# Two small unused tiles shift the places of a weight ring in SBUF

## The chip, the cores and the metric

The kernel runs on one core of one Trainium2 chip. The metric is the device time of one launch in microseconds (us). Before the change it is 1526.59 us, the median of three runs (1525.78 to 1528.01). The execution that the profiler recorded took 1525.17 us, of which the recorded span of instructions is 1523.3 us.

## The reference

Two residual layers act on x, 256 tokens of 1024 channels in float32. Each layer has a token mixer and a channel mixer. In layer 0 the channel mixer is a dense SwiGLU, in layer 1 it is a sum over eight experts of which each token uses two:

```
for l in range(DEPTH):                                   # 2 layers
    ada = cs @ ada_w[l] + ada_b[l]                       # six vectors that scale and shift
    h = rmsnorm(x, norm_mix_g[l]) * (1.0 + sc1) + sh1
    x = x + g1 * token_mixer(h, ...)                     # recurrence and attention, 9 projections
    h = rmsnorm(x, norm_ffn_g[l]) * (1.0 + sc2) + sh2
    f = swiglu(h, w1, w3, w2) if l % 2 == 0 else moe_swiglu(h, router, w1, w3, w2)
    x = x + g2 * f
...
for e in range(N_EXPERTS):                               # in moe_swiglu
    out = out + comb[:, e:e + 1] * swiglu(t, w1[e], w3[e], w2[e])
```

An expert has two matrices of 1024 x 3584 and one of 3584 x 1024, together 42 MB (here and below one MB of a load is 1024 KB, as the profile's list of DMAs counts). All eight are read once: 336 MB of the weights that the kernel reads.

## The kernel before

Every weight passes through a ring of buffers in SBUF and is read from there by TensorE. A load is one DMA of 1 MB into a place of 8192 bytes on each of the 128 partitions; `load` (lines 115 to 124) issues it from SyncE's queue. In the layers before the experts the ring is the pool `rawp` with 6 places (`RAW_BUFS`, line 33), and `split` (line 132) turns each tile into a high and a low part `wh` and `wl`, which are places of 4096 bytes in the pool `splp`.

In the expert stage (`moe`, line 757) nothing is split. The ring has 16 places there (line 1040), which `ahead` (line 1042) fills in a fixed rotation:

- places 0 to 5: the 6 places of `rawp`, here called the first ring;
- places 6 to 10: 5 places `raw2` of the expert stage's own pool, the second ring (`RAW_MORE`);
- place 11: the two tiles `xT`, which hold half a load each;
- places 12 to 15: the 4 + 4 places of `wh` and `wl`, again half a load each.

```
slots_ = RAW_BUFS + RAW_MORE + 1 + SPLIT_BUFS                         # line 1040
src, turn_ = plan[len(loaded)](), len(loaded) % slots_                # line 1045
halves = [xt.rearrange("p k t -> p (k t)") for xt in xT]              # line 1049, place 11
halves = [splp.tile([P, 1024], F32, tag=tag, ...) for tag in ("wh", "wl")]  # line 1051, places 12 to 15
load(src, raw, k=k)                                                   # line 1057, a whole load
nc.sync.dma_start(half.rearrange("p (k f) -> p k f", k=k // 2), part) # line 1063, a half load
```

So a row of the profile with SyncE's line L120 is a whole load into one of the two rings, and L1063 is a half load (or the two halves of the last unit).

An expert is worked in four units. Units 0 to 2 take 1024 columns of the hidden width, unit 3 takes 512. A unit's `up` (line 1074) reads 8 loads (unit 3: 4) of the first two matrices and `down` (line 1121) reads 4 loads (unit 3: 2) of the third. What stands in one unbroken run of bytes differs: an `up` load of units 0 to 2 brings runs of 4096 bytes, one of unit 3 runs of 2048 bytes, and a `down` load runs of 8192 bytes, or 4096 where it is cut into halves. An expert thus has 24 loads of 4096-byte runs, 4 of 2048 and 14 of 8192. Half of the experts are held for up to 96 tokens, half for up to 64 (`CAPS`, line 35). An expert of 96 tokens needs a third group of matmuls for each load (L1092, L1138); one of 64 does not.

The order of the work is this. SyncE issues the loads in the order of `plan` (line 1030). It waits for TensorE to release the place of 16 loads earlier, and no more than 8 DMAs stand in the queue, since 8 semaphores tell of landings in turn. TensorE consumes the loads in the same order. Which engine waits is decided by whether the next load has landed.

The places themselves come from the order in which tiles and pools are made. The pool `const` lies first, then `keep`, `hp`, `gp`, `rawp`, `splp`, and behind these the pools of the single stages.

Of the kernel before, what the change touches and what calls it, by code (L numbers as in the profile page):

```python
# [8 lines left out]
F32 = mybir.dt.float32  # L9
# [8 lines left out]
P = 128  # L18
# [30 lines left out]
def hybrid_trunk(ctx: ExitStack, tc: tile.TileContext, x, c, ada_w, ada_b, norm_mix_g, norm_ffn_g, w_in, lb_logits,  # L49
# [7 lines left out]
    const = ctx.enter_context(tc.tile_pool(name="const", bufs=1))  # L57
# [14 lines left out]
    def nm(s):  # L72
        uid[0] += 1
        return f"{s}_{uid[0]}"
# [18 lines left out]
    def ms():  # L93
        return msp.tile([P, 512], F32, tag="ms", name=nm("ms"))
# [6 lines left out]
    def small(shape, name, dt=F32, bufs=None, pool=None):  # L101
        return (pool or phase[0]).tile(shape, dt, tag=name, name=nm(name), **({"bufs": bufs} if bufs else {}))
# [56 lines left out]

    xT = [const.tile([P, 4, S], F32, name=f"xT{h}") for h in range(2)]  # L160
    ident = const.tile([P, P], F32, name="ident")
    cT = const.tile([P, KD], F32, name="cT")
    nc.sync.dma_start(cT, c.rearrange("o (p k) -> (o p) k", k=KD))
    first_phase = ExitStack()
# [592 lines left out]
    def moe(y, l, pdp):  # L757
# [12 lines left out]
        nc.sync.dma_start(row, ada_b[l, 4096:].rearrange("(q f) -> q f", q=4).unsqueeze(1).broadcast_to((4, 32, 512)))  # L770
        v_.tensor_tensor(row, row, ada[l, 2]["row"], op=ALU.add)
        lp = [ms() for _ in range(NT)]
        xs = [small([P, D], "xs") for _ in range(NT)]
        begun = set()
        xg = [small([P, D], "xg") for _ in range(NT)]
# [481 lines left out]
    for l in range(DEPTH):  # L1257
# [23 lines left out]
        if l % 2 == 0:  # L1281
            with new_phase("ffn"):
                gain = pcol[:, R_FFN + 8 * l:R_FFN + 8 * l + 8]
                sc, sh = ada[l, 2]["col"][:, 0:8], ada[l, 1]["col"][:, 8:16]
                early, then = unnormed(gain, sc, sh)
                acc = end_of_mixer(then)
                queue(*QUEUES[2 * l + 1])
                if l == 0:
                    fillers.append(late_constants)
                filling[:] = -DELAYS[2 * l + 1], RATES[2 * l + 1]  # L1290
                rb = in_sbuf(norm_rows(acc))
                acc, early = dense_ffn(early, rb, lambda: norm_T(rb, gain, sc, sh), l)
                while fillers:
                    fillers.pop(0)()
        else:
            before_experts.close()
            turn_mm[0] = -(1 << 30)
            with tc.tile_pool(name="pdp", bufs=2, space=PSUM) as pdp, new_phase("moe"):
                moe(y, l, pdp)
# [57 lines left out]
```

## Time and profile before

| what | value |
|---|---|
| median of 3 runs | 1526.59 us |
| profiled execution | 1525.17 us, its span 1523.3 us |
| TensorE (PE) busy | 1470.4 us, 97% of the span |
| VectorE (DVE), ScalarE (ACT) busy | 629.3 us (41%), 373.9 us (25%) |
| DMA | 506.62 MB (10^6 bytes) in 186032 packets, mean 333 GB/s |
| share of the chain that ended last | PE 83%, DMA 9%, issue 5% |

The span has four parts. Up to about 34 us the first scale and shift vectors are formed. From there to about 600 us stand the layers' projections, which TensorE does nearly without a gap at about 240 GB/s of DMA. To about 668 us follow the last projection and the router. From 668 to 1510 us the experts run: TensorE is nearly full and the DMA engines move about 410 GB/s all the while. An engine's busy time counts each matmul with a modelled end, so a short wait of TensorE may show as busy.

### The profile page before, as it was taken

What the parts mean: (1) busy time and instruction counts of PE and PEld (TensorE: products, weight loads), DVE (VectorE), ACT (ScalarE), POOL (GpSimd) and SP (SyncE); (2) the same over time, 40 slices, a digit from 0 to 9 for tenths busy, and PEclk for the clock granted to TensorE, in tenths of its full rate; (3) what the DMA queues carried; (4) which work ended last, traced back from release to release, by engine and by line L of the source; (5) the groups of instructions that cost most, each with busy time, mean ns of one, the idle gap of its engine ahead of it and who ended that gap; (6) DMA issues with size and microseconds to landing.
All of it is one profiled execution on the core that took longest, in us unless ns stands there. A gap on an engine that the chain in (4) does not pass through costs nothing.

```text
span 1523.3 us, 29680 instructions
## 1 busy us (share of the span) xinstructions
PE 1470.4 (97%) x12659; PEld 893.8 (59%) x12659; DVE 629.3 (41%) x1046; ACT 373.9 (25%) x618; POOL 33.9 (2%) x34
## 2 busy tenths in 40 slices
PE   5999999999999999999999999999999998999996
PEld 3988999999998899863333333433334332234322
DVE  4898777877688887631100211120011120111202
ACT  3535556544455455310000000000000000000000
POOL 1010100000000100000000000000000000000000
PEclk7999999999999999899999999999999999999999
DMA  9988545678896555868999999999999999999996
GB/s 356 369 303 282 189 139 166 222 237 302 267 342 227 194 178 200 293 229 321 408 412 413 410 416 411 415 415 410 410 415 411 412 417 408 413 406 409 412 416 250
DMA packets 186032, 506.62 MB, mean 333 GB/s; under 512 B 11016, under 2 KB 79252, under 8 KB 170148
## 3 DMA queue, kind: packets, MB, share of 16 engines
q1 hardware_dynamic: 185572, 504.56, 86.7%
q8 instruction: 101, 1.65, 0.4%
q14 instruction: 39, 0.32, 0.1%
q0 software_dynamic: 320, 0.09, 0.0%
HBM read 503.56 MB, written 1.05 MB: 331 GB/s over the span
## 4 chain that ended last, share of the span: by engine, by line
PE 83%; DMA 9%; issue 5%; DVE 1%; SPq 1%; ACT 1%; POOL 0%; DVEq 0%; POOLq 0%; ACTq 0%
PE mm L157 31%; PE mm L1087 23%; DMA raw<-in_moe_w_dram 8%; PE pd L1132 6%; PE at L1092 6%; PE pd L1138 4%; PE at L1132 4%; PE ms L862 2%; PE ms L530 2%; DMA raw<-in_ada_w_dram 1%; PE ms L1114 1%; PE ms L1176 1%; PE ada L227 1%; PE at L613 1%; DVE wl L148 0%
## 5 line engine op out<-in xcount | busy, mean ns | idle before, releaser
L1087 PE MATMUL mm<-raw,X 128*32 128x512 f32 (+1 forms) x3792 | 441.4, 543 | 3.9 <-DMA raw<-in_moe_w_dram 3.8
L1087 PEld LDWEIGHTS mm<-raw,X 128*32 128x32 f32 x3792 | 132.2, 110 | 227.3 <-issue 190.4
L148 DVE TENSOR_TENSOR wl<-raw,wh 128x1024 fp32r<-128x1024 f32 (+1 forms) x188 | 226.6, 1209 | 74.9 <-ACT wh L146 72.5
L146 ACT ACTIVATE wh<-raw 128x1024 fp32r<-128x1024 f32 (+1 forms) x188 | 196.6, 1048 | 176.9 <-PE mm L157 133.9
L1099 DVE TENSOR_TENSOR sa<-sa,mm 128x512 f32<-128x512 f32 (+1 forms) x32 | 19.9, 621 | 472.1 <-PE mm L1087 396.2
L1092 PE MATMUL at<-raw,X 128*32 128x512 f32 (+1 forms) x952 | 172.2, 542 | 0.0
L157 PE MATMUL mm<-hh,wh 128*128 128x256 f32 x576 | 164.1, 285 | 3.4 <-ACT wh L146 3.1
L157 PE MATMUL mm<-hl,wh 128*128 128x256 f32 x576 | 164.7, 286 | 0.0
L157 PE MATMUL mm<-hh,wl 128*128 128x256 f32 x576 | 164.5, 286 | 0.1
L1098 ACT ACTIVATE sa<-mm 128x512 f32<-128x512 f32 (+1 forms) x32 | 17.4, 544 | 522.9 <-PE mm L1087 522.9
L1132 PE MATMUL pd<-raw,u 128*32 128x512 f32 x848 | 121.5, 594 | 0.0
L157 PEld LDWEIGHTS mm<-hh,wh 128*128 128x128 f32 x576 | 109.9, 191 | 5.6 <-ACT wh L146 3.5
L157 PEld LDWEIGHTS mm<-hl,wh 128*128 128x128 f32 x576 | 109.5, 190 | 0.7 <-issue 0.7
L157 PEld LDWEIGHTS mm<-hh,wl 128*128 128x128 f32 x576 | 109.3, 190 | 0.4 <-DVE wl L148 0.4
L1132 PE MATMUL at<-raw,u 128*32 128x512 f32 x816 | 95.1, 594 | 12.2 <-DMA raw<-in_moe_w_dram 12.0
L1138 PE MATMUL pd<-raw,u 128*32 128x512 f32 x424 | 87.4, 592 | 0.0
L1092 PEld LDWEIGHTS at<-raw,X 128*32 128x32 f32 x952 | 46.5, 110 | 61.1 <-issue 55.1
L221 DVE SCALAR_TENSOR_TENSOR raw<-raw,cs,raw 128x2048 f32<-128x2048 f32 x32 | 75.1, 2346 | 8.9 <-DMA raw<-in_ada_w_dram 8.9
L1132 PEld LDWEIGHTS at<-raw,u 128*32 128x32 f32 x816 | 25.5, 109 | 71.8 <-issue 46.0
L157 PE MATMUL mm<-wh,hh 128*128 128x512 f32 x160 | 64.6, 404 | 0.0
L157 PE MATMUL mm<-wl,hh 128*128 128x512 f32 x160 | 64.0, 400 | 0.0
L1132 PEld LDWEIGHTS pd<-raw,u 128*32 128x32 f32 x848 | 31.3, 110 | 54.7 <-issue 51.0
(308 smaller groups left out, 2038.3 us busy)
## 6 DMA issues: line engine op xcount, KB each, us to landing
raw<-in_moe_w_dram SPq DMA_DIRECT2D x231, 1024.0 KB, 15.7
raw<-in_moe_w_dram SPq DMA_DIRECT2D x168, 512.0 KB, 11.2
raw<-in_ada_w_dram SPq DMA_DIRECT2D x47, 1024.0 KB, 4.9
raw<-in_w_in_dram SPq DMA_DIRECT2D x44, 1024.0 KB, 7.5
raw<-in_ffn_w_dram SPq DMA_DIRECT2D x30, 1024.0 KB, 5.2
xT<-in_moe_w_dram SPq DMA_DIRECT2D x42, 512.0 KB, 16.5
raw<-in_w_out_dram SPq DMA_DIRECT2D x8, 1024.0 KB, 5.0
raw<-in_w_branch_a_dram SPq DMA_DIRECT2D x4, 1024.0 KB, 5.4
```

Of the source, the lines that this page charges most:

```text
L146: s_.activation(wh[:, c], r[:, c], AF.Copy)
L148: v_.tensor_tensor(wl[:, c], r[:, c], wh[:, c].bitcast(F32), op=ALU.subtract)
L157: t_.matmul(ps, lhsT=lhs, rhs=rhs, start=first and i == 0, stop=last and i == 2)
L221: v_.scalar_tensor_tensor(got["acc"], raw, cs[:, k:k + 1], got["acc"], op0=ALU.mult, op1=ALU.add)
L530: t_.matmul(ps[:, at_:at_ + HD].rearrange("p (g w) -> p g w", w=H), lhsT=kq[:, h, i * P:(i + 1) * P], rhs=rhs, start=True, stop=True)
L862: t_.matmul(ps[:, i * n:(i + 1) * n], lhsT=xg[t][:, k * P:(k + 1) * P], rhs=pm[:, t, :n], start=t == 0, stop=t == NT - 1)
L1087: t_.matmul(ups[m][q:q + 32, :n], lhsT=xp[:, k, 32 * s:32 * s + 32], rhs=rhs[m][h], start=k == 0, stop=k == KD - 1)
L1092: t_.matmul(ups[2][q:q + 32, :n], lhsT=xp[:, k, 64:96], rhs=rhs[m][h], start=k == 0, stop=k == KD - 1)
L1098: s_.activation(sv, in_order(ups[0][:, :n]), AF.Silu)
L1099: v_.tensor_tensor(sv, sv, in_order(ups[1][:, :n]), op=ALU.mult)
L1132: t_.matmul(dn[0][q:q + 32, :], lhsT=us[0][:, k, 64 * h + 32 * s:64 * h + 32 * s + 32], rhs=rhs[h][c], start=first and h == 0, stop=last a ...
L1138: t_.matmul(dn[1][q:q + 32, :], lhsT=us[1][:, k, 32 * h:32 * h + 32], rhs=rhs[h][c], start=first, stop=last)
```

## The change

Two tiles are allocated that nothing writes or reads: 480 bytes per partition in `const`, after `ident`, and 32 bytes in the expert stage's pool, ahead of `xs`.

```
     xT = [const.tile([P, 4, S], F32, name=f"xT{h}") for h in range(2)]
     ident = const.tile([P, P], F32, name="ident")
+
+    const.tile([P, 120], F32, name="gap")
     cT = const.tile([P, KD], F32, name="cT")
...
         lp = [ms() for _ in range(NT)]
+        small([P, 8], "gap", bufs=1)
         xs = [small([P, D], "xs") for _ in range(NT)]
```

The instructions, their order on every engine and the semaphores that they wait for are the same in both kernels; addresses alone differ. All SBUF tiles made after `ident` move by 480 bytes, and those of the expert stage's pool from `xs` on by 512. The start of a place on its partition, as a remainder on division by 512:

| places | before | after |
|---|---|---|
| first ring, 6 places (the first at byte 67616, then 68096) | 32 | 0 |
| `wh` and `wl`, 8 places of half a load | 32 | 0 |
| second ring, 5 places (the first at byte 177664, then 178176) | 0 | 0 |
| `xT`, 2 places of half a load | 128 | 128 |
| `x_in`, the two tiles that take x | 416 and 0 | 384 and 480 |

Of the other tiles some that stood at a multiple of 64 bytes now stand 32 past one, and the reverse.

## Rows read from the trace of the kernel before

**Rows 1.** Windows: length, busy us (instructions) by engine, PE clock, DMA share, GB/s.

```profile
34.00:600.00 566.00, 562.94 (x4224) 527.81 (x4225) 453.63 (x648) 289.92 (x472) 26.95 (x18) 0.99 0.70 243
...
668.00:1060.00 392.00, 390.79 (x3717) 142.09 (x3720) 58.59 (x138) 23.98 (x43) 0.00 (x0) 1.00 0.98 391
1060.00:1110.00 50.00, 45.42 (x442) 18.25 (x434) 5.28 (x8) 2.58 (x5) 0.00 (x0) 1.00 1.02 411
1110.00:1260.00 150.00, 149.12 (x1384) 53.32 (x1386) 22.62 (x48) 8.96 (x16) 0.00 (x0) 1.00 1.02 414
1260.00:1320.00 60.00, 53.05 (x530) 17.23 (x524) 3.86 (x6) 3.15 (x6) 0.00 (x0) 1.00 1.02 408
1320.00:1460.00 140.00, 139.12 (x1302) 49.98 (x1300) 21.14 (x38) 9.59 (x17) 0.00 (x0) 1.00 1.02 410
1460.00:1510.00 50.00, 43.31 (x434) 14.11 (x428) 5.96 (x9) 2.59 (x5) 0.00 (x0) 1.00 0.95 379
```

**Rows 2.** Waits of PE, then of PEld, 668 to 1510 us: total us, times, longest.

```profile
PE at L1132 <- DMA raw<-in_moe_w_dram: 12.0, 11, 1.6
...
PE mm L1087 <- DMA raw<-in_moe_w_dram: 3.8, 6, 0.8
...
PEld at L1132 <- DMA raw<-in_moe_w_dram: 25.0, 25, 2.5
PEld mm L1087 <- DMA raw<-in_moe_w_dram: 19.8, 45, 1.4
```

**Rows 3.** Timeline of PE, 1264 to 1316 us: start, us, what, [idle before, releaser].

```profile
1274.22 1.93 PE L1087 MATMUL mm<-raw,X 128*32 128x256 f32 x32 [0.68 <-DMA raw<-in_moe_w_dram]
...
1279.51 1.93 PE L1087 MATMUL mm<-raw,X 128*32 128x256 f32 x32 [0.73 <-DMA raw<-in_moe_w_dram]
...
1284.53 3.64 PE L1132 MATMUL at<-raw,u 128*32 128x512 f32 x32 [1.04 <-DMA raw<-in_moe_w_dram]
1289.43 2.78 PE L1132 MATMUL at<-raw,u 128*32 128x512 f32 x24 [1.26 <-DMA raw<-in_moe_w_dram]
```

**Rows 4.** Timeline of PE, 1464 to 1512 us.

```profile
1479.00 3.64 PE L1132 MATMUL at<-raw,u 128*32 128x512 f32 x32 [0.75 <-DMA raw<-in_moe_w_dram]
...
1483.99 3.64 PE L1132 MATMUL at<-raw,u 128*32 128x512 f32 x32 [1.34 <-DMA raw<-in_moe_w_dram]
...
1488.86 3.64 PE L1132 MATMUL at<-raw,u 128*32 128x512 f32 x32 [1.24 <-DMA raw<-in_moe_w_dram]
```

**Rows 5.** Timeline of SyncE, three single loads: start of the issue.

```profile
847.93 0.38 SPq L120 DMA_DIRECT2D raw<-in_moe_w_dram  x1
...
851.86 0.37 SPq L120 DMA_DIRECT2D raw<-in_moe_w_dram  x1
...
859.59 2.85 SPq L120 DMA_DIRECT2D raw<-in_moe_w_dram  x1
```

**Rows 6.** DMA list, the same three issues: KB, last number us to landing.

```profile
raw<-in_moe_w_dram SPq DMA_DIRECT2D x1, 1024.0 KB, 15.0
...
raw<-in_moe_w_dram SPq DMA_DIRECT2D x1, 1024.0 KB, 18.7
...
raw<-in_moe_w_dram SPq DMA_DIRECT2D x1, 1024.0 KB, 18.3
```

**Rows 7.** DMA issues of the page: count, KB each, median us to landing.

```profile
raw<-in_moe_w_dram SPq DMA_DIRECT2D x231, 1024.0 KB, 15.7
raw<-in_moe_w_dram SPq DMA_DIRECT2D x168, 512.0 KB, 11.2
...
xT<-in_moe_w_dram SPq DMA_DIRECT2D x42, 512.0 KB, 16.5
```

**Rows 8.** The chain that ended last, 0 to 100 us: start, us.

```profile
4.46 12.39 DMA raw<-in_ada_w_dram
...
19.70 9.91 DMA raw<-in_ada_w_dram
```

**Rows 9.** Line L650: duration ns minimum/median/maximum.

```profile
L650 ACT ACTIVATE gt<-mm x32: 358/384/388, 144.0 to 598.7; 128x256 f32<-128x256 f32 x32
```

More of the change, by code (lines that the diff above doesn't have):

```diff
@@ L161, in hybrid_trunk @@
     ident = const.tile([P, P], F32, name="ident")
+    const.tile([P, 120], F32, name="gap")
     cT = const.tile([P, KD], F32, name="cT")
@@ L772, in moe @@
         lp = [ms() for _ in range(NT)]
+        small([P, 8], "gap", bufs=1)
         xs = [small([P, D], "xs") for _ in range(NT)]
```

## The prediction

> **What bounds the kernel now.** I read the windows by stage first, then TensorE's waits, then its timeline in the places where it waits, and last the landings of single loads.
>
> In the windows [rows 1] compare the length with PE's busy time. From 34 to 600 us PE is idle for 566.0 - 562.9 = 3.1 us and the DMA engines have room (share 0.70): faster loads are worth nothing there. In the expert stage, 668 to 1510 us, the DMA share is about 1.0 in every window, and PE's idle time sits in three of them: 4.6 us in 1060 to 1110, 6.9 in 1260 to 1320 and 6.7 in 1460 to 1510, while the 682 us between lack only 3.0 in all. Both engines are nearly full, in turns: an expert of 96 tokens keeps TensorE busy for longer than its loads take, one of 64 for less, and where the 16 loads of lead are used up TensorE waits.
>
> What it waits for is the weights: 12.0 + 3.8 = 15.8 us of PE's idle time ends with a landing [rows 2]. That understates the waits, because a matmul's modelled end covers the first part of each. In [rows 4] 32 records are drawn as 3.64 us; 1483.99 and 1488.86 follow landings. The queue of weight loads, which has no such tail, shows 25.0 + 19.8 = 44.8 us in 70 waits [rows 2], and these include the ordinary space between two weight loads. So the waits for weights are worth between 15.8 and 44.8 us. I take 25: about 16 plus some 0.13 us for each of the 70. Spread over the three stretches in the ratio of their idle times this is 6, 10 and 9 us.
>
> **The change, part by part.** No instruction, wait or order changes, and the two new tiles cost nothing by themselves. What changes is where loads are written: the first ring and the split places go from 32 bytes past a multiple of 512 to a multiple of it. The kernel before already has both kinds, since the second ring starts at multiples of 512. So the trace has the price of the change in it: how fast loads land back to back on either kind.
>
> Runs of 8192 bytes: 1479.00 to 1483.99 is the wait for two loads onto the first ring, 4.99 / 2 = 2.495 us each; 1483.99 to 1488.86 two loads onto the second, 4.87 / 2 = 2.435 [rows 4]. In [rows 3] 1284.53 to 1289.43 are two more onto the second, 4.90 / 2 = 2.45. The difference is 0.05 us a load.
>
> Runs of 4096 bytes: of the three loads in [rows 5, 6] the first lands at 847.93 + 15.0 = 862.93, the second at 851.86 + 18.7 = 870.56 and the third at 859.59 + 18.3 = 877.89. Three loads land onto the first ring between the first and the second, 7.63 / 3 = 2.54 us each, and three onto the second ring from there to the third, 7.33 / 3 = 2.44. The difference is 0.10 us, good to about 0.03, as the list has one decimal.
>
> Runs of 2048 bytes: 1274.22 to 1279.51 are two loads onto the first ring, 5.29 / 2 = 2.645 us [rows 3]. The four loads that follow, with longer runs, land on the second ring in 1289.43 - 1279.51 = 9.92, or 2.48 each. The difference is 0.165 us; no row has this run on the second ring alone, so it may be from 0.1 to 0.2.
>
> Each price is nearly the same for each run: 1 MB over 16 engines is 64 KB an engine, which is 8, 16 or 32 runs, and 0.05 / 8, 0.10 / 16 and 0.165 / 32 are 6, 6 and 5 ns. That speaks for a fixed cost of each run that starts askew.
>
> [...]
>
> How many loads: 231 whole ones, of which 6 in 11 or 126 go to the first ring; the 168 halves are 84 MB in split places [rows 7]. The 105 of the second ring and the 21 MB in `xT` keep their remainder, so they gain nothing. With 24, 4 and 14 loads of 42 by run, the first ring saves 72 x 0.10 + 12 x 0.165 + 42 x 0.05 = 11.3 us. In split places the 8192-byte runs are cut to 4096, so 76 x 0.10 + 8 x 0.165 = 8.9. Together 20.2 us of DMA time, nearly 1.0 us for each of the 21 rotations of 16 loads; a rotation lasts 16.8 MB (10^6) at 411 GB/s = 41 us.
>
> What of it reaches the end: only what shortens a wait, and what is saved while TensorE is the bound is held at most as a fuller ring. Before 1060 us some 8 rotations save 8 us, against waits of 6 in the first stretch: all 6 go, and about 2 are carried on. From 1060 to the end of the second stretch at 1320 lie 6.3 rotations: 6.3 + 2 = 8.3 against 10, so 8.3 go. From 1320 to 1510 lie 4.6: 4.6 against 9, so 4.6 go, and waits of about 6 us stay in the last two stretches. The sum is 6 + 8.3 + 4.6 = 18.9; some gaps of the queue behind a slow release stay, so I take 18.5.
>
> Ahead of the experts: the first 34 us hang on loads of `ada_w` for 12.39 + 9.91 us of the chain [rows 8]. Seven are of 8192-byte runs, 7 x 0.05 = 0.35; the eighth is cut to 1024-byte runs, 64 x 5 ns = 0.3. One tile of x loses its multiple of 512, half a load at 0.1 a load: 0.05. That is 0.6 us, bounded by 0 and 1. The end, behind 1510 us, has no load of weights.
>
> The sum against the profiled execution: 1525.17 - 18.5 - 0.6 = 1506.1. The median of the runs stands 1.4 above that execution, so 1507.5.
>
> **Rivals.** *Half the price.* The split places, or the longest runs, do not answer as the first ring does: no row compares halves on both kinds of place. Without the 8.9 us of the split places a rotation saves 0.55 us. Then 4.4, 3.5 and 2.5 go, 10.4, and the time is about 1516. Against it speaks that the price is one of each run, whatever the tile.
>
> *The small price.* A run that starts 32 bytes askew may cost only the time of 32 bytes more, and the rest of the difference may belong to the second ring for another reason (where it lies in SBUF, or its turn in the rotation). At 2.44 us for 4096-byte runs that is 2.44 x 32 / 4096 = 0.02 us a load, 4 us on the 126 + 84 loads that move: 1522. [...] Against it: the same 6 ns a run comes out at three lengths and at three moments.
>
> *No change.* The engines may be held by what HBM gives over a whole rotation, so that the second ring is only fast behind a slow stretch. Then 1526.6. Against it: 2.44 us is held for three loads in a row [rows 5, 6] and 2.48 for four [rows 3], far more than the engines could hold back.
>
> *Slower.* All weight places start at the same remainder, and the DMA writes come faster beside matmuls that read SBUF; if these meet in the memory, TensorE's steps stretch. It is busy for 821 us of the 842 between 668 and 1510 (the six windows of [rows 1]), so 2.3% on that would eat the 19 us, and from there on the change is a loss; at 3.5% it adds 29 and the time is 1536. Against it: 32 records of L1132 take 3.64 us from the first ring (1479.00) and from the second (1488.86) alike [rows 4]. ScalarE also writes `gt` to tiles at both kinds of start, a multiple of 64 bytes and 32 past one, and its 32 instructions lie between 358 and 388 ns, with the median at 384 [rows 9].
>
> [...]
>
> **How the numbers follow.** My forecast has 0.77, at 1502 to 1513: with waits of 22 or 30 us in place of 25 the first two stretches give 2 us less or more, and with prices off by a quarter the sum moves by 4. Half the price has 0.10, the small price 0.05, no change 0.05, slower 0.03. The range from 1501 to 1515 holds the forecast and the near part of the half. A measurement here can tell 0.2% or 3 us from no change. Faster by more than that: 0.77 + 0.10 + 0.05 = 0.92. Within it: 0.05. Slower: 0.03.
>
> **What would show it.** In the profile after, a load onto the first ring lands in 2.44 to 2.48 us where the engines are full, and 4096-byte runs no longer differ between the rings. The DMA rate in full windows rises from 408 to 414 GB/s to about 420. PE's idle time falls to nearly none around 1060, by more than half in the second stretch, and by half in the third; a matmul keeps its length. The last load lands about 19 us sooner, and up to 600 us nothing moves by more than 1 us. If the landings come closer and the end does not, I was wrong on the waits; if the first ring stays at 2.54, on the cause.

## The result and the profile after

The changed kernel takes 1515.35 us in the median of 6 runs (1513.55 to 1517.2), the kernel before 1528.2 in the median of 6. The ratio is 0.9915 (95% interval 0.9905 to 0.9925): 13.0 us less (11.5 to 14.5). In a second comparison (e7 below) it was 0.992 (0.9904 to 0.9935). The forecast was 19.1 us less, 1507.5 with a range up to 1515.0: the direction was right, the size was not. A ratio is not the quotient of the two medians, so the two can differ by some tenths of a us, and by 2 us in e8.

The recorded execution of the change is its slowest, 1517.2 us with a span of 1515.4; that of e7, the same kernel, has a span of 1512.5. The windows below are of the changed kernel, in the stretches of [rows 1], with the same columns; the last begins 9 us earlier, as its work does.

```profile
34.00:600.00 566.00, 563.16 (x4211) 528.41 (x4212) 452.20 (x645) 287.86 (x469) 26.35 (x18) 0.99 0.69 242
...
668.00:1060.00 392.00, 390.79 (x3704) 142.43 (x3707) 59.34 (x141) 23.97 (x43) 0.00 (x0) 0.99 0.97 394
1060.00:1110.00 50.00, 48.54 (x482) 20.48 (x470) 6.57 (x10) 2.58 (x5) 0.00 (x0) 1.00 1.02 416
1110.00:1260.00 150.00, 149.12 (x1392) 53.32 (x1390) 21.70 (x47) 9.56 (x17) 0.00 (x0) 1.00 1.02 417
1260.00:1320.00 60.00, 55.07 (x550) 19.14 (x548) 5.64 (x9) 3.18 (x6) 0.00 (x0) 1.00 1.02 417
1320.00:1460.00 140.00, 139.12 (x1318) 50.13 (x1314) 19.04 (x34) 8.96 (x16) 0.00 (x0) 1.00 1.02 416
...
1451.00:1501.00 50.00, 45.04 (x454) 14.90 (x448) 5.97 (x9) 2.59 (x5) 0.00 (x0) 1.00 0.95 384
```

Up to 600 us nothing changed. TensorE's idle time fell from 4.6 to 1.5 us in 1060 to 1110, but from 6.9 to 4.9 only in 1260 to 1320, where the forecast had left less than 2 us of 10. In the third stretch it fell from 6.7 to 5.0, a quarter and not the half of the forecast. The DMA engines move 416 to 417 GB/s in place of 408 to 414, not the 420 of the forecast. TensorE's work is unchanged: in the windows from 1110 and from 1320, where it does not wait, it is idle for the same 0.9 us as before.

The expert stage from its first to its last weight matmul, before and after (the lines are three further down: L1090 was L1087, L1135 was L1132, L1194 was L1191):

```profile
672.54 1.05 PE L1087 MATMUL mm<-raw,X 128*32 128x512 f32 x6
...
1508.47 3.73 PE L1191 MATMUL pd<-raw,u 128*32 128x512 f32 x32 [0.53 <-ACT u L1116]
```

```profile
673.32 1.07 PE L1090 MATMUL mm<-raw,X 128*32 128x512 f32 x8
...
1499.51 3.94 PE L1194 MATMUL pd<-raw,u 128*32 128x512 f32 x32 [0.53 <-ACT u L1119]
```

That is 839.7 us before and 830.1 after, 9.5 less (e7: 830.3). The last load landed at 1501.5 us in place of 1510.2, 8.8 sooner (e7: 12.2), where the forecast had 19.

TensorE's waits for weights, as in [rows 2]:

```profile
PE at L1135 <- DMA raw<-in_moe_w_dram: 6.7, 7, 1.3
...
PE mm L1090 <- DMA raw<-in_moe_w_dram: 2.1, 2, 1.6
...
PEld at L1135 <- DMA raw<-in_moe_w_dram: 18.6, 25, 2.2
...
PEld mm L1090 <- DMA raw<-in_moe_w_dram: 15.3, 44, 2.1
```

PE's idle time behind a landing went from 15.8 to 8.8 us, that of the weight-load queue from 44.8 to 33.9. Where I take, for each first use of a load that starts within 0.9 us of its landing, the step to it less an ordinary step of 0.21 us, the waits are about 26 us before, 15 after and 16 in e7. No view prints these sums; they are worked out from the trace's single records and good to some 3 us.

How fast do loads land now? Over all loads of 4096-byte runs the median interval between two landings is 2.481 us on the first ring and 2.484 on the second, where it was 2.557 and 2.455: as forecast, the rings no longer differ. The timeline of PE in the second stretch of waits, to be read against [rows 3], shows two loads of 8192-byte runs between its rows: 1279.19 to 1284.08 is 4.89 / 2 = 2.445 us a load, on the second ring, as before.

```profile
1279.19 3.64 PE L1135 MATMUL at<-raw,u 128*32 128x512 f32 x32 [0.90 <-DMA raw<-in_moe_w_dram]
1284.08 2.78 PE L1135 MATMUL at<-raw,u 128*32 128x512 f32 x24 [1.24 <-DMA raw<-in_moe_w_dram]
```

The three loads of [rows 5, 6] in e7, SyncE's rows first and the DMA list behind them. By the landings' own stamps (859.40, 866.82 and 874.30 us; the list rounds to 0.1) the three loads onto the first ring took 2.47 us each and the three onto the second 2.49. Before they took 2.55 and 2.44, by stamps as well.

```profile
845.84 0.38 SPq L120 DMA_DIRECT2D raw<-in_moe_w_dram  x1
...
849.58 0.37 SPq L120 DMA_DIRECT2D raw<-in_moe_w_dram  x1
...
856.97 2.09 SPq L120 DMA_DIRECT2D raw<-in_moe_w_dram  x1
```

```profile
raw<-in_moe_w_dram SPq DMA_DIRECT2D x1, 1024.0 KB, 13.6
...
raw<-in_moe_w_dram SPq DMA_DIRECT2D x1, 1024.0 KB, 17.2
...
raw<-in_moe_w_dram SPq DMA_DIRECT2D x1, 1024.0 KB, 17.3
```

So in these loads the first ring gained 0.08 and the second ring, which still starts at multiples of 512, lost 0.05. That loss is what the experiments had to explain.

### The profile page after: what moved, and what is told of

It reads as the page before. It is cut to its first block, busy times and chain, and to the rows that moved or that the text cites. A ratio compares the mean times of both kernels' runs of the same rounds, so it can differ in the third digit from the quotient of the medians.

```text
span 1515.4 us, 29680 instructions
## 1 busy us (share of the span) xinstructions
PE 1468.2 (97%) x12659; PEld 897.3 (59%) x12659; DVE 629.6 (42%) x1046; ACT 374.0 (25%) x618; POOL 33.8 (2%) x34
## 4 chain that ended last, share of the span: by engine, by line
PE 85%; DMA 7%; issue 5%; DVE 1%; SPq 1%; ACT 1%; POOL 0%; DVEq 0%; POOLq 0%; ACTq 0%
PE mm L157 32%; PE mm L1090 24%; PE pd L1135 6%; DMA raw<-in_moe_w_dram 6%; PE at L1095 6%; PE at L1135 4%; PE pd L1141 4%; PE ms L865 2%; PE ms L532 2%; PE ms L1117 1%; DMA raw<-in_ada_w_dram 1%; PE ms L1179 1%; PE ada L229 1%; PE at L615 1%; DVE wl L148 0%
## 5 line engine op out<-in xcount | busy, mean ns | idle before, releaser
L1090 PE MATMUL mm<-raw,X 128*32 128x512 f32 (+1 forms) x3792 | 439.8, 543 | 2.2 <-DMA raw<-in_moe_w_dram 2.1
L1090 PEld LDWEIGHTS mm<-raw,X 128*32 128x32 f32 x3792 | 133.0, 110 | 223.1 <-issue 189.8
L1135 PE MATMUL pd<-raw,u 128*32 128x512 f32 x848 | 121.5, 594 | 0.0
L1135 PE MATMUL at<-raw,u 128*32 128x512 f32 x816 | 94.0, 594 | 7.0 <-DMA raw<-in_moe_w_dram 6.7
L1135 PEld LDWEIGHTS at<-raw,u 128*32 128x32 f32 x816 | 25.7, 110 | 65.3 <-issue 46.3
L1135 PEld LDWEIGHTS pd<-raw,u 128*32 128x32 f32 x848 | 31.3, 110 | 54.7 <-issue 51.2
```

Of the source, the lines that this page charges most:

```text
L1090: t_.matmul(ups[m][q:q + 32, :n], lhsT=xp[:, k, 32 * s:32 * s + 32], rhs=rhs[m][h], start=k == 0, stop=k == KD - 1)
L1135: t_.matmul(dn[0][q:q + 32, :], lhsT=us[0][:, k, 64 * h + 32 * s:64 * h + 32 * s + 32], rhs=rhs[h][c], start=first and h == 0, stop=last a ...
```

## The experiments

The time of each is set against the kernel before on the same chip; e5 and e9 are one recorded execution each. Askew means a start that is no multiple of 256 bytes, 32 past one where nothing else is said. Two theories stood against each other. A: a run of bytes that starts askew costs its own time, whatever lands around it. B: the second ring's 2.44 us was in part a catching up behind slower writes, and no rate that lasts.

**e1: the second ring askew as well.** Of the change's two tiles, only the second is there:

```
         lp = [ms() for _ in range(NT)]
+        small([P, 8], "gap", bufs=1)
```

Expected: 

> The second ring goes to 32 bytes past a multiple of 512 as well, so 15 of the 16 load places are askew (xT stays at 128). Theory A (each askew run costs its own time, whatever its neighbours): the 105 MB of the second ring lose 60 x 0.10 + 10 x 0.165 + 35 x 0.05 = 9.4 us of DMA time, and its 4096-byte loads land in 2.55 us in place of 2.45. TensorE waits for most of that: 1534 to 1538 against 1528. Theory B (what lands fast on the second ring is in part a catching up behind slower writes): the loads all land at the rate of writes that are askew, the same 2.55; also 1534 to 1538. Rival (the second ring is fast for where it lies, not for its remainder): 1528, and 2.45 on it.

Measured: ratio 1.0059 (1.0046 to 1.0073), 1536.51 against 1527.25 us. The waits for weights, worked out as above, rose from about 26 to 38 us. On the timeline of PE, two loads of 8192-byte runs onto the second ring stand between these rows: 5.02 / 2 = 2.51 us each, where the kernel before had 2.45 [rows 3].

```profile
1294.16 3.64 PE L1133 MATMUL at<-raw,u 128*32 128x512 f32 x32 [1.01 <-DMA raw<-in_moe_w_dram]
1299.18 2.78 PE L1133 MATMUL at<-raw,u 128*32 128x512 f32 x24 [1.38 <-DMA raw<-in_moe_w_dram]
```

So the start's remainder sets the second ring's rate (2.45 us a load at a multiple, 2.51 at 32 past), and not where the ring lies in SBUF. In this place 32 unused bytes cost 9 us.

**e2: all at 64 past a multiple of 512.** Gap tiles of 32 and 32 bytes:

```
+    const.tile([P, 8], F32, name="gap")
...
+        small([P, 8], "gap", bufs=1)
```

Expected: 

> Both rings and the split places stand 64 bytes past a multiple of 512; the gap tiles are 32 and 32 bytes. If only the remainder by 64 matters, this is as fast as the change itself, 1514 to 1517. If it takes a multiple of 128, 256 or 512, the second ring becomes askew too and the time is that of the kernel with all places askew, 1534 to 1538.

Measured: 1.0053 (1.004 to 1.0067), 1535.31 against 1527.25 us, as slow as e1. A multiple of 64 is not enough.

**e3: the first ring alone.** The change's first tile, and one of 32 bytes at the head of the pool `splp`:

```
+    const.tile([P, 120], F32, name="gap")
...
     splp = ctx.enter_context(tc.tile_pool(name="splp", bufs=SPLIT_BUFS))
+    splp.tile([P, 8], F32, name="gap_s", bufs=1)
```

Expected: 

> The first ring goes to a multiple of 512 and the split places stay 32 past one; the second ring is at a multiple. Theory A (prices add up): this is the first ring's share of the change, 11.3 of 20.2 parts of 12.9 us, so 7 us faster than before: 1521. Theory B (loads at a multiple land faster among slow ones, as reads run ahead there): the first ring gains its full 0.10 us for each 4096-byte load, 0.55 us a rotation, 10 us: 1518, and this and the next kernel together gain more than the change, some 18 us.

Measured: 0.9965 (0.9952 to 0.9978), 5.3 us less.

**e4: the split places alone.** No tile in `const`, 480 bytes in `splp`, 32 in the expert stage's pool:

```
+    splp.tile([P, 120], F32, name="gap_s", bufs=1)
...
+        small([P, 8], "gap", bufs=1)
```

Expected: 

> Only the split places go to a multiple of 512; the first ring stays 32 past one, the second ring at a multiple. Theory A: 8.9 of 20.2 parts of 12.9 us, 6 us faster: 1522. Theory B: the full 0.44 us a rotation, 8 us: 1520. If halves of loads do not answer to their place: 1528.

Measured: 0.9956 (0.994 to 0.9971), 6.7 us less. The split places answer, so the rival *half the price* falls, though its 1516 is the number nearest to the result. e3 and e4 add up to 12.0 us, good to about 3, which is the change: the times are those of theory A, and what I expected of B, 18 us together, did not come. The landings, though, were B's. The medians of the intervals between landings of 4096-byte loads were 2.557 us on the first ring and 2.455 on the second before; in e3 they were 2.455 on the first and 2.482 on the second. The ring that comes first behind askew places is the fast one. My sum for B was wrong: the kernel before has that gain already, so moving the first ring only takes it over from the second.

**e5: the price by itself.** All computation is left out. SyncE issues loads of 1 MB into 8 places, 24 for each run and start, and 48 in the pattern of the ring before:

```
    MIX = (32,) * 6 + (0,) * 6 + (32,) * 4
    for dst, src in loads(4096, (0,), 24):
        nc.sync.dma_start(dst, src)
    for dst, src in loads(4096, (32,), 24):
        nc.sync.dma_start(dst, src)
    ...
    for dst, src in loads(4096, MIX, 48):
        nc.sync.dma_start(dst, src)
```

Expected: 

> This kernel leaves the whole computation out: SyncE alone issues loads of 1 MB of expert weights, 24 in a row for each length of run and start of the place, and 48 in the pattern of the ring before (6 loads at 32 bytes past a multiple of 512, 6 at a multiple, 4 at 32 past). Nothing waits but for the load of 8 before. Theory A (each askew run costs its own time): 4096-byte runs take 2.45 us a load at a multiple and 2.55 at 32 past, in the pattern as in the pure stretches; 8192-byte runs 2.44 and 2.49. Theory B (writes at a multiple are held by the reading side, which runs ahead behind slow writes): pure 4096-byte runs at a multiple take 2.48 us, 2048-byte runs 2.56, 8192-byte runs 2.445, while in the pattern the loads at a multiple land in 2.45. Pure runs at 32 past take 2.555 and 2.69 by both. At 64 past as at 32 past; at 256 past as at a multiple if the step is 256.

Measured: the windows of the run, each from the landing of a stretch's first load to that of its last, so that the length over 23 (over 47 in the last row) is the time of a load. In order: 8192-byte runs at a multiple of 512 and at 32 past; 4096, 2048 and 1024 the same; 4096 at 64, at 128 and at 256 past; the pattern.

```profile
5.78:62.20 56.42, 0.00 (x0) 1.00 1.01 427
64.70:122.05 57.35, 0.00 (x0) 1.00 1.01 420
124.50:181.69 57.19, 0.00 (x0) 1.00 1.03 421
184.78:243.65 58.87, 0.00 (x0) 1.00 1.02 410
246.12:305.07 58.95, 0.00 (x0) 1.00 1.05 409
307.78:370.09 62.31, 0.00 (x0) 1.00 1.04 387
372.65:435.14 62.49, 0.00 (x0) 1.00 1.09 386
438.16:507.43 69.27, 0.00 (x0) 1.00 1.09 350
509.99:569.57 59.58, 0.00 (x0) 1.00 1.02 409
572.12:630.97 58.85, 0.00 (x0) 1.00 1.03 410
633.41:690.61 57.20, 0.00 (x0) 1.00 1.03 421
693.18:811.80 118.62, 0.00 (x0) 1.00 1.03 416
```

| run | at a multiple | 32 past | difference | by run (8, 16, 32, 64 an engine) |
|---|---|---|---|---|
| 8192 bytes | 2.453 us | 2.493 us | 0.040 us | 5.0 ns |
| 4096 bytes | 2.487 us | 2.560 us | 0.073 us | 4.6 ns |
| 2048 bytes | 2.563 us | 2.709 us | 0.146 us | 4.6 ns |
| 1024 bytes | 2.717 us | 3.011 us | 0.294 us | 4.6 ns |

The prediction had 0.05, 0.10 and 0.165 for the first three. At a multiple theory A had expected 2.44 us for 8192-byte runs and 2.45 for 4096, theory B 2.445 and 2.48, and 2.56 for 2048: B's are the nearer. The rival *the small price*, 0.02 us a load, falls. The 59.58 us at 64 past hold one step of 3.26 us; the other 22 steps are 2.56 us, as at 32 past. That 2.44 is no rate that lasts is shown by the landings of the pattern: behind the six askew loads the six at a multiple came at intervals of 2.44, 2.45, 2.45, 2.47, 2.50 and 2.50 us. The pure stretch of 4096-byte runs at a multiple began behind askew ones too, with 2.45, 2.45, 2.47 and 2.49, and then stayed at 2.49 to 2.50. So the quick landings last for three loads, and the three loads of [rows 5, 6] are just those.

Did the bytes come faster as well? The same pattern, cut at landings: three quick loads, the three behind them, then two askew ones and seven more askew.

```profile
705.97:713.30 7.33, 0.00 (x0) 1.00 1.02 420
713.30:720.77 7.47, 0.00 (x0) 1.00 1.03 421
720.77:725.91 5.14, 0.00 (x0) 1.00 1.03 418
725.91:743.82 17.91, 0.00 (x0) 1.00 1.03 410
```

They did not. Three loads of 1 MB landing in 7.33 us are 429 GB/s, and 420 were moved, the rate of the pure stretch (421): for three loads the landings gain on the packets. Behind them it is the reverse, two askew loads land at 408 GB/s while 418 are moved. A packet, which is one run here, took 159 ns at a multiple, in the quick loads too, and 163.4 on average at 32 past, by the trace's packet records. What a whole rotation of 16 loads wins by the mixture is little: 40.4 us from landing to landing, where the pure rates make 6 x 2.487 + 10 x 2.560 = 40.5.

**e6, e7, e8: xT as well, the change again, and 256.** e6 is the change with 384 bytes ahead of `xT` and 96 behind `ident`, so that all 16 places are at multiples of 512. e7 is the changed kernel. e8 has gaps of 224 and 32 bytes, so that both rings and the split places are 256 past.

```
+    const.tile([P, 96], F32, name="gap_x")       # e6, ahead of xT
+    const.tile([P, 24], F32, name="gap")         # e6, behind ident
+        small([P, 8], "gap", bufs=1)             # e6, e8
+    const.tile([P, 56], F32, name="gap")         # e8, behind ident
```

Expected of e6: 

> The change with the two xT tiles at a multiple of 512 as well, so that all 16 places of the expert stage are. If a start at 128 costs what one at 32 or 64 costs, the 21 MB in xT save about 0.08 us each, 1.7 us, and this is 1513 to 1514.5 where the change gives 1515.3. If 128 is as good as 512: the same as the change.

Expected of e7: 

> The changed kernel itself, beside the others on one chip: 1513 to 1517, and its PE waits for weights in the expert stage are again near 15 us of the 26 before, in the same three stretches. If the profile of the change was a slow one of its kind, waits of 10 to 13 us.

Expected of e8: 

> Both rings and the split places stand 256 past a multiple of 512. [...] If it takes 512: 1534 to 1538, as with all places at 64.

Measured: 0.9922 (0.9905 to 0.9939), 0.992 (0.9904 to 0.9935) and 0.9921 (0.9902 to 0.994). The three cannot be told apart. What e6 gains over the change, 1.7 us by my expectation, is smaller than the intervals show, so there is no version here that beats the change. For e8, a multiple of 256 is enough, as in e5: 57.20 us at 256 past against 57.19 at 512, while 64 past (without its one long step) and 128 past cost 2.56 us a load. The price is 0.073 us in 2.487, nearly 3%, and it does not grow with the bytes ahead of the start: 32, 64 and 128 past cost the same. Why the step is at 256 was not shown.

**e9: the loads of four experts, by themselves.** All computation is left out. The kernel's plan of loads, halves included, is issued with the starts of before and then with those of the change. In the trace the second stretch has the same loads in another order: in each rotation places 8 to 15 come ahead of 0 to 7.

```
    for dst, src in loads(32, 0, 128, 32):      # first ring, second ring, xT, split places
        nc.sync.dma_start(dst, src)
    for dst, src in loads(0, 0, 128, 0):
        nc.sync.dma_start(dst, src)
```

Expected: 

> This kernel leaves the whole computation out: SyncE issues the loads of four experts in the order of the kernel's plan, halves included, first with the starts of the kernel before (first ring and split places 32 past a multiple of 512, second ring at one, xT at 128 past), then with those of the change. Four experts are 168 loads, 10.5 rotations. By the prices of the prediction the second stretch is 0.96 us a rotation shorter, 10.1 us; by the pure stretches of the run before (0.073, 0.146 and 0.04 us for runs of 4096, 2048 and 8192 bytes) 0.73 us a rotation, 7.7 us. If halves do not answer to their place: 4.3 us.

Measured: the windows from the first landing to the last of either stretch.

```profile
6.03:429.18 423.15, 0.00 (x0) 1.00 1.02 415
431.63:848.19 416.56, 0.00 (x0) 1.00 1.02 421
```

Each stretch holds one step of about 3.2 us in place of some 2.5; these cancel to about 0.3 us. The change saves 423.15 - 416.56 = 6.6 us for four experts, or 0.63 us a rotation, 13.2 us for eight: neither 10.1 nor 7.7 for the four. The pure prices give 0.73, and they too are not paid in full, since the five loads of the second ring landed quickly before: about 2.9 of them in a rotation have 4096-byte runs and lose 0.036 (medians 2.455 and 2.491 us in this run), half a one has 2048-byte runs and loses 0.035, together 0.1.

**e10: what the waits are worth.** In the kernel before, `xT` is not loaded again from load 32 on, so its place's matmuls read old values:

```
                         halves = [xt.rearrange("p k t -> p (k t)") for xt in xT]
+                        if len(loaded) >= 32:
+                            loaded.append(halves)
+                            continue
```

Expected: 

> The kernel before, but from load 32 on the place xT is not loaded again (TensorE reads what stands there), so some 19 MB of the 336 are left out. That takes about 48 us from the DMA engines and nothing from TensorE's work, though its order shifts in places. What TensorE waits for weights goes almost entirely, and the time falls by that: if the 25 us that the prediction took are right, to 1501 to 1504; if the waits are only the idle time of 15.8 us, to 1511; if they are near the 44.8 us of the weight-load queue, below 1490.

Measured: 0.9845 (0.9829 to 0.9861), 1504.22 against 1527.69 us: 23.7 us less (21 to 26). No idle time of PE behind a landing is left, as its list of waits from 668 to 1490 us shows; the weight-load queue, below it, keeps 11.8 us in 40 waits, none over 0.4, which include the ordinary space between two weight loads (before: 44.8 us, up to 2.5 [rows 2]).

```profile
PE ms L1117 <- DVE sa L1102: 2.1, 3, 0.9
PE pd L1194 <- ACT u L1119: 0.5, 1, 0.5
PE ms L862 <- DVE pm L855: 0.3, 1, 0.3
```

```profile
PEld mm L1090 <- DMA raw<-in_moe_w_dram: 9.1, 31, 0.4
...
PEld at L1135 <- DMA raw<-in_moe_w_dram: 2.1, 7, 0.3
...
PEld pd L1135 <- DMA raw<-in_moe_w_dram: 0.6, 2, 0.3
```

So the waits could give 21 to 26 us. The 25 of the prediction lies within that, if near its upper end: 1504.22 is just above the 1501 to 1504 expected for it, and in the recorded execution the expert stage is 20.6 us shorter than before. Some of TensorE's instructions stand in another order in this kernel, so a small part of it may be from that.

## Why the prediction was right in direction and wrong in size

- **The bound.** Right: both engines are nearly full in turns (in the changed kernel TensorE is idle for 0.9 us in each of the windows from 1110 and 1320, and the DMA share there is 1.02), TensorE waits in three stretches (1.5, 4.9 and 5.0 us idle after the change), and e10 puts the waits at 23.7 us (21 to 26) where 25 was taken.
- **The mechanism.** Right: a start that is no multiple slows the load, in the second ring (e1, 9.3 us slower), the first (5.3 us gained in e3) and the split places (6.7 us gained in e4), and by a cost of each run that is nearly the same at four lengths (4.6 to 5.0 ns in e5).
- **The price.** This step failed: "Three loads land onto the first ring between the first and the second, 7.63 / 3 = 2.54 us each, and three onto the second ring from there to the third, 7.33 / 3 = 2.44. The difference is 0.10 us". Askew was right, 2.56 in e5. At a multiple the rate that lasts is 2.49; 2.44 is that of the first landings behind askew loads. The price is 0.073, and 0.04 and 0.146 in place of 0.05 and 0.165. With them the 20.2 us of DMA time become 72 x 0.073 + 12 x 0.146 + 42 x 0.04 + 76 x 0.073 + 8 x 0.146 = 15.4. The same error put a term at nothing: "The 105 of the second ring and the 21 MB in `xT` keep their remainder, so they gain nothing". The second ring loses by the change, and what is left of the 15.4 is 13.2 (e9).
- **The rival that I dismissed.** *No change* named what the landings showed, a second ring that is "only fast behind a slow stretch"; that HBM holds the engines, its reason, was not shown. I held three loads in a row at 2.44 against it and called that "far more than the engines could hold back". In e5 three loads in a row landed at 2.44 to 2.45 us, while the bytes moved at 420 GB/s as later. The rival's end, 1526.6, is wrong, but the quick landings account for most of the 7.0 us of DMA time that the forecast had too much.
- **What reaches the end.** With 0.63 us a rotation in the prediction's own rule, 8 rotations give 5.0 of the first stretch's 6 us, 6.3 give 4.0 of the second's 10 and 4.6 give 2.9 of the third's 9. The sum is 11.9, with the early term 12.5; measured are 13.0, and 12.2 in the second comparison. The recorded executions give less: the expert stage is 9.5 us shorter (9.4 in e7), and waits of 13 us should stay, where about 15 and 16 did. So the rule may give some 2 us too much. The kernel before has one recorded execution, 3 us below its median, and where the rest of the 13 us lies stays open.
- **Ahead of the experts.** The term of 0.6 us was about right: the chain's `ada_w` part ended at 29.61 us before [rows 8] and at 28.81 after, in the row below. It was 28.51 in e7, 28.63 in e3, and 29.53, 29.96 and 29.81 in e1, e2 and e4, where the first ring is askew. The start of the expert stage scatters by more, from 670.1 to 674.0 us over the recorded executions, so it cannot be followed to the end.

```profile
19.75 9.06 DMA raw<-in_ada_w_dram
```

- **Slower.** Nothing of it came: 32 records of L1135 take 3.64 us after as before, with all the places of both rings alike.
- **The range.** Its upper end, 1515.0, stood for price errors of a quarter. The prices took a quarter off the 20.2 us of DMA time and the second ring's loss another tenth; the median lies 0.35 us past the end.

Why the landings gain on the packets for three loads, and no longer, was not shown. Nor was theory B's reason, slower writes that are caught up with: no run separated reads from writes.

## What to carry to other kernels

Put the places in SBUF that loads are written to at a multiple of 256 bytes where loads bound the kernel: here it took 3% off a load of 4096-byte runs (2.560 to 2.487 us in e5), and 13 us off 1528. A rate read from a few transfers in a mixed pattern is no lasting rate, since landings can gain on the bytes moved for a few loads and lose again (in e5 429 GB/s landed and 420 moved for three loads, later 408 and 418 for two); look whether the interval still drifts within the group, or run the pure pattern by itself. Price a change that speeds a shared queue by what the whole rotation gains, with the places that do not move in the sum.

## What the runs showed of the hardware that was not expected

- A run costs time even at a multiple: loads of 8192, 4096, 2048 and 1024-byte runs took 2.453, 2.487, 2.563 and 2.717 us for 1 MB (the last from landings at 372.65 and 435.14 us, 62.49 / 23). That is 4.2, 4.8 and 4.8 ns for each run more on an engine. An askew start costs 4.6 to 5.0 ns again, as much as one run more; why was not shown. The runs of different length also come from different places in HBM, which no run held apart.
- Starts 32, 64 and 128 past cost the same, 2.56 us a load (e5, 64 past without one step of 3.26 us), and 256 past costs nothing. By the packet records a 4096-byte run took 159 ns at a multiple of 256, and 163.4, 163.4 and 163.6 on average at 32, 64 and 128 past.
- In the first three loads behind askew ones, loads at a multiple landed in 2.45 us in place of 2.49, while the bytes moved at the same 420 to 421 GB/s as later (e5).
